# A first stage in two passes of four units, with twelve modulation tiles on TensorE

## The chip, the cores and the metric

The kernel runs on one core of one Trainium2 chip. The metric is the device time of one execution in microseconds. Engines are called TensorE (PE in the profile, PEld for its weight loads), VectorE (DVE), ScalarE (ACT), GpSimd (POOL) and SyncE (SP, whose queue issues the DMAs).

## What is computed

Two residual blocks over 512 tokens of width 2048, the first with two layers and a context of 256 tokens. All of it is fp32. Cut to what the change touches:

```
for l in range(DEPTH):
    sh_l, sc_l, g_l = jnp.split(jax.nn.silu(c) @ w_mod[l] + b_mod[l], 3, axis=-1)
    sh_c, sc_c, g_c = jnp.split(jax.nn.silu(c_ctx) @ w_mod[l] + b_mod[l], 3, axis=-1)
    hl = xl * (1.0 + sc_l[:, None, :]) + sh_l[:, None, :]
    hc = xc * (1.0 + sc_c) + sh_c
    parts_l = jnp.split(hl @ w_in[l], SPLIT_POINTS, axis=-1)
    ...
y_conv = jax.nn.silu(g) * (b_gate * conv3(c_gate * u))
y_pool = jax.nn.silu(g) * (einsum(window_mean(u) - u, pool_w) * pool_scale)
out = jnp.concatenate([y_conv, y_attn, y_pool], axis=-1) @ w_out_l
```

A shift, scale or gate is a vector of 2048 numbers per sequence: a product of silu(c) with a 2048x6144 matrix. The columns of that matrix come in 48 tiles of 128 (0 to 15 shift, 16 to 31 scale, 32 to 47 gate).

## The kernel before

**Matrix products.** Every fp32 operand of a product is split into a high part (a cast to fp32r) and a low part (the rest), and a product is three matmuls: high by high, high by low, low by high. A *unit* is one tile of 128 columns of `w_in`: 16 k-steps, in each three matmuls over the 512 rows of the latent sequence (into `u.lat`) and three over the 256 rows of the context (into `u.cx`). `load_chunk` fetches the weights: DMA to `wraw` on SyncE's queue, cast to `whi` on ScalarE, subtraction to `wlo` on GpSimd. `H[k]` and `Hc[k]` hold the rows in both parts.

**Dots.** A modulation value is a dot of 2048 numbers per partition. In the first stage `gemv` and `dot` make them from a whole tile `wm` (128x2048 fp32, 1 MB): one operation with a running sum on VectorE (L292), or, for the second vector of every odd tile, a product on GpSimd (L288) and a sum on ScalarE (L289). Later stages do them in quarters of 512 in the background (`dots`, `along`: so many steps per finished unit, put late by the scheduler): on GpSimd and ScalarE during attention (L797, L798), on VectorE in the conv and pool branch (L801).

**The first stage** (`pool("start")`, 0 to 325 us) runs three passes over the 16 k-steps. Pass 1, five units (the gates of the four pool tiles and the first conv gate): per k-step two dots for the scale, the rows times (1 + scale) without the shift (L743), split into parts (L713 and L139), then `side_steps` with the matmuls (L240 latent, L241 context). The missing shift is added to those gates later: `pgb` holds the product of the shift with the gate columns. Pass 2, three units (the other conv gates), no new rows; the 32 dots of the shift run beside it. Pass 3 adds the shift to the rows (L761), splits them again, and makes the four units of head 0. The gates go to DRAM (`PGd`) through `pg` (L754, L755).

**Attention of layer 0** (to about 1084 us): 27 units and eight heads; in the background the eight gates' shift products and 16 tiles of layer 0.

**The branch** (to about 1358 us) goes conv 0, pool 0, conv 1, pool 1, conv 2, pool 2, pool 3, conv 3. A conv tile j has units j (copied to `uu`), 8+j (times `uu` into `V`, three taps into `yc`) and 4+j (times `yc`), then its gate from DRAM (`early_gate`, L499), tanh, a last product (L530) and `yc` to DRAM. A pool tile sums windows on GpSimd, makes `dd` (L560, L561), casts to `dh` on ScalarE (L564), makes `dl` on GpSimd, and multiplies by `pool_w` on TensorE into `ps_v`; `yp` (L579) takes that out. `dd` and `yp` share the one buffer of `yc`, `U` that of `V`. PSUM has four `ps_m` buffers, two per unit with context.

The order on each engine is set when the program is built, by a scheduler with priorities; each engine then runs its own queue in order.

## Time and profile before

| what | us |
|---|---|
| median of three runs | 3625.3 (3614.6 to 3630.26) |
| the profiled execution | 3616.4 |
| its span, first to last instruction | 3614.7 |
| TensorE busy | 3270.7 |
| VectorE busy | 2482.0 |
| first stage | 0 to 325.3 |
| branch of layer 0 | 1083.8 to 1358.0 |

Busy times are of one execution. Matmuls are pipelined and their ends are modelled, so the time of a stretch of matmuls is read from the starts of two of them and not from their lengths. A group with "idle before" shows what the engine waited for ahead of these instructions. PEclk is the granted clock of TensorE as a share of 2.4 GHz (its other level is 1.2 GHz).

### The profile page before, as it was taken

The page shows a single profiled execution, that of the slowest core. Times are in us where ns is not written, and L with a number is a line of the kernel's source. Part 1 is how long each engine was busy: PE and PEld are TensorE (multiplying, and loading weights), DVE is VectorE, ACT ScalarE, POOL GpSimd, SP SyncE. Part 2 cuts the span into 40 slices and gives each one's busy share as a digit, 9 for nine tenths or more (in the row PEclk, how much of TensorE's full clock was granted, in tenths as well). Part 3 has the DMA queues.
Part 4 walks back from the last instruction along what each step waited for, and adds up shares of the span by engine and source line. Part 5 has one row for each costly group of instructions (what it writes and reads, how often), then busy time and mean ns, then how long its engine had stood idle before and what let it go on. Part 6 is the DMA issues. An engine that isn't in the chain of part 4 may idle for free.

```text
span 3614.7 us, 47947 instructions
## 1 busy us (share of the span) xinstructions
PE 3270.7 (90%) x16462; PEld 2740.4 (76%) x16462; DVE 2482.0 (69%) x3785; ACT 1545.9 (43%) x3208; POOL 2064.5 (57%) x1452
## 2 busy tenths in 40 slices
PE   5769899989998879889999999999989899999997
PEld 4668788878886767668888888877768787787765
DVE  9994555555547998874466655486477899986676
ACT  4433656666542113233566664322445333245343
POOL 5665677777423443255877773488776544444432
PEclk8889999999999989999999999999999999999998
DMA  7542333333215557664655552487776222223575
GB/s 260 198 174 87 107 108 101 111 107 105 72 65 181 175 162 236 202 212 142 169 148 148 149 149 76 148 302 245 236 225 199 88 87 89 85 82 102 183 223 186
DMA packets 271700, 553.61 MB, mean 153 GB/s; under 512 B 30592, under 2 KB 37600, under 8 KB 263264
## 3 DMA queue, kind: packets, MB, share of 16 engines
q1 hardware_dynamic: 268896, 537.97, 46.3%
q0 software_dynamic: 2560, 12.58, 1.7%
q8 instruction: 129, 2.11, 0.2%
q14 instruction: 115, 0.94, 0.1%
HBM read 508.05 MB, written 29.80 MB: 149 GB/s over the span
## 4 chain that ended last, share of the span: by engine, by line
PE 43%; DVE 27%; DMA 12%; issue 8%; POOL 6%; ACT 5%; SPq 0%; DVEq 0%; POOLq 0%; ACTq 0%
PE ps_m L166 32%; DMA wraw<-in_w_out_dram 5%; DVE acc L980 5%; DVE gpr L801 4%; DVE gjunk L292 2%; POOL gpr L797 2%; DVE wlo L139 2%; PE ps_s L389 2%; POOL wlo L139 2%; PE ps_v L428 2%; DVE h L139 2%; ACT whi L159 2%; DMA gv<-in_cc_dram 1%; DVE wm L292 1%; DVE hf L761 1%
## 5 line engine op out<-in xcount | busy, mean ns | idle before, releaser
L139 POOL TENSOR_TENSOR wlo<-wraw,whi 128x512 fp32r<-128x512 f32 x760 | 1115.6, 1485 | 876.0 <-ACT whi L159 763.3
L166 PE MATMUL ps_m<-h,whi 128*128 128x512 f32 (+1 forms) x4608 | 1569.3, 399 | 36.2 <-ACT vT L355 27.7
L166 PEld LDWEIGHTS ps_m<-h,whi 128*128 128x128 f32 x4608 | 875.4, 192 | 224.3 <-ACT vT L355 30.0
L159 ACT CAST whi<-wraw 128x512 fp32r<-128x512 f32 x1032 | 603.5, 618 | 779.1 <-DMA wraw<-in_w_out_dram 272.8
L166 PE MATMUL ps_m<-h,wlo 128*128 128x512 f32 (+1 forms) x2304 | 916.9, 398 | 0.1
L797 POOL TENSOR_TENSOR gpr<-gw,gv 128x512 f32<-128x512 f32 x320 | 425.3, 1329 | 227.9 <-ACT gpr L798 161.4
L166 PE MATMUL ps_m<-hc,whi 128*128 128x256 f32 x1920 | 518.5, 284 | 0.0
L166 PEld LDWEIGHTS ps_m<-h,wlo 128*128 128x128 f32 x2304 | 442.0, 192 | 93.8 <-POOL wlo L139 0.4
L139 DVE TENSOR_TENSOR wlo<-wraw,whi 128x512 fp32r<-128x512 f32 x272 | 242.5, 905 | 185.2 <-ACT whi L159 184.8
L166 PEld LDWEIGHTS ps_m<-hc,whi 128*128 128x128 f32 x1920 | 359.3, 191 | 3.9
L798 ACT ACTIVATE gpr<-gpr 128x512 f32<-128x512 f32 x320 | 201.9, 631 | 247.3 <-POOL gpr L797 246.6
L166 PE MATMUL ps_m<-hc,wlo 128*128 128x256 f32 x960 | 271.7, 283 | 0.0
L801 DVE SCALAR_TENSOR_TENSOR gpr<-gw,gv 128x512 f32<-128x512 f32 x264 | 255.6, 968 | 11.4 <-DMA gw<-in_w_mod_dram 3.0
L980 DVE SCALAR_TENSOR_TENSOR acc<-gu,pack,acc 128x511 f32<-128x511 f32 (+24 forms) x240 | 232.1, 979 | 5.4
L619 PE MATMUL ps_m<-wlo,y 128*128 128x512 f32 x512 | 206.2, 403 | 21.6 <-POOL wlo L139 12.6
L394 DVE TENSOR_REDUCE mx<-ps_s 128x1 f32<-128x768 f32 (+1 forms) x160 | 134.8, 842 | 114.1 <-PE ps_s L389 112.7
L620 PE MATMUL ps_m<-whi,y 128*128 128x512 f32 x512 | 202.2, 396 | 2.2 <-DVE y L139 1.6
L166 PEld LDWEIGHTS ps_m<-hc,wlo 128*128 128x128 f32 x960 | 183.4, 191 | 0.8
L618 PE MATMUL ps_m<-whi,y 128*128 128x512 f32 x512 | 181.3, 396 | 1.0 <-ACT whi L159 1.0
L423 DVE TENSOR_TENSOR aTl<-ps_t,aTh 128x384 fp32r<-128x384 f32 (+1 forms) x144 | 77.3, 537 | 151.9 <-ACT aTh L422 151.6
L240 PE MATMUL ps_m<-h,whi 128*128 128x512 f32 x320 | 125.4, 439 | 58.9 <-DVE h L139 30.3
L389 PE MATMUL ps_s<-K,Q 128*128 128x384 f32 x576 | 134.2, 348 | 7.9 <-ACT E L403 6.1
(370 smaller groups left out, 5622.0 us busy)
## 6 DMA issues: line engine op xcount, KB each, us to landing
wraw<-in_w_in_dram SPq DMA_DIRECT2D x640, 256.0 KB, 3.0
wraw<-in_w_out_dram SPq DMA_DIRECT2D x384, 256.0 KB, 3.5
wm<-in_w_mod_dram SPq DMA_DIRECT2D x48, 1024.0 KB, 5.8
gw<-in_w_mod_dram SPq DMA_DIRECT2D x192, 256.0 KB, 3.5
gw<-in_w_ada_dram SPq DMA_DIRECT2D x136, 256.0 KB, 3.3
wm<-in_w_ada_dram SPq DMA_DIRECT2D x14, 1024.0 KB, 5.2
K<-K POOLq DMA_DIRECT2D x32, 384.0 KB, 4.1
yraw<-yd SPq DMA_DIRECT2D x40, 256.0 KB, 3.5
```

The lines of the kernel that those rows point to most:

```text
L139: eng.tensor_tensor(lo, src, hi.bitcast(F32), op=ALU.subtract)
L159: nc.scalar.copy(hi[:, sl], raw)
L166: nc.tensor.matmul(ps, w, mv[part], start=(first and p == 0), stop=(last and p == 2))
L389: nc.tensor.matmul(o, Qm[:, q0:q0 + 128], kp[:, c * ncol:(c + 1) * ncol], start=i == 0, stop=i == 1)
L394: nc.vector.reduce_max(mx, sv, axis=AX.XY)
L618: nc.tensor.matmul(ps, yh, hi[:, sl], start=(k == 0), stop=False)
L619: nc.tensor.matmul(ps, yh, lo[:, sl], start=False, stop=False)
L620: nc.tensor.matmul(ps, yl, hi[:, sl], start=False, stop=(k == KT - 1))
L797: nc.gpsimd.tensor_tensor(pr, w, t, op=ALU.mult)
L798: nc.scalar.activation(pr, pr, AF.Copy, scale=scale, accum_out=part[v][:, i:i + 1])
L801: nc.vector.scalar_tensor_tensor(junk, w, scale, t, op0=ALU.mult, op1=ALU.mult, accum_out=part[v][:, i:i + 1])
L980: nc.vector.scalar_tensor_tensor(A[:, s:], U[:, :NL - s], wj(i), A[:, s:], op0=ALU.mult, op1=ALU.add)
```

## The change

The first stage has two passes of four units. Pass 1 makes the four pool gates from the scaled rows, pass 2 the four units of head 0 from shifted rows. The four conv gates become plain units inside `conv_tile`. Twelve of the 32 modulation tiles (0, 4, 8, 12 and the even ones from 16 to 30) are laid out as they stand in `w_mod`, and TensorE makes their 128x2 values for both vectors in 16 fp32 matmuls with two columns each; the other 20 tiles are dots on VectorE for both vectors. In pass 1 the rows are scaled straight into the high part on ScalarE, and the low part is one operation on VectorE (L739 of the new file). In pass 2 the x tiles are loaded a second time, ScalarE scales and shifts them, casts the high part, and the low part goes to VectorE (512 columns) and GpSimd (256). `wm` has four buffers instead of three. Behind it, `pgb` has four gates instead of eight, four tiles of layer 1 move from the branch to attention, and the branch takes 6 background steps per unit instead of 10.

```diff
+PE_TILES = (0, 4, 8, 12) + tuple(range(16, 32, 2))
...
-    GATES = (52, 53, 54, 55, 12, 13, 14, 15)
+    GATES = (52, 53, 54, 55)
...
-        gate = early_gate(xp, 4 + j) if l == 0 else unit(w, 12 + j, H, cx)
+        gate = unit(w, 12 + j, H, cx)
         for o, vo, n in seqs:
             th = xp.tile([128, NL], F32, name="th", tag="th", bufs=2)
-            silu2(th[:, :n], gate[:, o:o + n] if l == 0 else pt(gate, o), th[:, :n])
+            silu2(th[:, :n], pt(gate, o), th[:, :n])
...
-        for p, (g0, n) in enumerate(((0, 5), (5, 3))):
...
-                        dot(sp, wm, (cl, cc_)[i], s1[i], last=i == 1, split=k % 2 == 1)
...
-                    gemv(sp, a["w_mod"][0][k], [(cl, "l0", "b_mod0", k), (cc_, "c0", "b_mod0", k)],
-                         wm_bufs=3, split=k % 2 == 1)
...
+        def columns(m, dst):
+
+            wm = load_gemv(sp, a["w_mod"][0][m], 4)
+            if m in PE_TILES:
+                ps = next(banks)()[:, :2]
+                for q in range(KT):
+                    nc.tensor.matmul(
+                        ps, wm[:, q * 128:(q + 1) * 128], cT[:, 2 * q:2 * q + 2], start=q == 0, stop=q == KT - 1
+                    )
+                return ps
+            if not vecs:
+                vecs.extend(cvecs(sp, 0, 1))
+            for i in range(2):
+                dot(sp, wm, vecs[i], dst[:, i:i + 1], last=i == 1)
+            return dst
...
+        def scaled_rows(k):
+            r = columns(16 + k, s1[:, k])
+            xr = load_x(k)
+            nc.vector.tensor_scalar(s1[:, k], r, P("b_mod0")[:, 16 + k:17 + k], 1.0, op0=ALU.add, op1=ALU.add)
+            for i, (nm, o, n, dst) in enumerate(halves):
+                nc.scalar.activation(dst[k][:, 0], xr[:, o:o + n], AF.Copy, scale=s1[:, k, i:i + 1])
+            for i, (nm, o, n, dst) in enumerate(halves):
                 nc.vector.scalar_tensor_tensor(
+                    dst[k][:, 1], xr[:, o:o + n], s1[:, k, i:i + 1], dst[k][:, 0].bitcast(F32),
+                    op0=ALU.mult, op1=ALU.subtract,
+                )
+
+        def shifted_rows(k):
+            r = columns(k, sh[:, k])
+            xr = load_x(k)
+            hf = sp.tile([128, NT], F32, name="hf0", tag="hf0", bufs=2)
+            nc.vector.tensor_scalar(sh[:, k], r, P("b_mod0")[:, k:k + 1], None, op0=ALU.add)
+            for i, (nm, o, n, dst) in enumerate(halves):
+                nc.scalar.activation(
+                    hf[:, o:o + n], xr[:, o:o + n], AF.Identity, scale=s1[:, k, i:i + 1], bias=sh[:, k, i:i + 1]
+                )
+                nc.scalar.copy(dst[k][:, 0], hf[:, o:o + n])
+                sub_lo(dst[k][:, 1], hf[:, o:o + n], dst[k][:, 0], nc.gpsimd if i else nc.vector)
+
+        def pass_(rows, ns, zero):
+            us, ch = side_units(zero), []
+            rows(0)
+            for k in range(KT):
+                if k < KT - 1:
+                    rows(k + 1)
+                side_steps(w0, ns, us, H, Hc, k, ch, zero)
+            return us
...
+        for g, u in enumerate(pass_(scaled_rows, GATES, zero)):
...
+        us = pass_(shifted_rows, (16, 24, 32, 40), zero)
...
-            dots(ap_, ("sh_l", "sh_c"), 1.0, [a["w_gateT"][g] for g in range(8)], [pgb[:, 0], pgb[:, 1]], 2, 1),
+            dots(ap_, ("sh_l", "sh_c"), 1.0, [a["w_gateT"][g] for g in range(4)], [pgb[:, 0], pgb[:, 1]], 2, 1),
             mod_dots1(ap_, 0, 32, 48, 2, 1),
+            mod_dots1(ap_, 1, 0, 4, 2, 1),
...
-        along(mod_dots1(gp, 1, 0, 20, 4), 10)
+        along(mod_dots1(gp, 1, 4, 20, 4), 6)
...
+    for m in PE_TILES:
+        a["w_mod"][0, m] = v["w_mod"][0][:, m * 128:(m + 1) * 128].reshape(16, 128, 128).transpose(1, 0, 2).reshape(128, 2048)
```

How the order on the engines moves is seen at three places.

VectorE in pass 1, k-steps 1 to 4, before. `gjunk` and `wm` are the outputs of the dots of the two vectors, `h` and `hc` the low parts of latent and context rows, `s` the scale:

```order
L292 SCALAR_TENSOR_TENSOR gjunk,s_389<-wm,ca_171 128x2048
L139 TENSOR_TENSOR hc_1_148<-hf_289,hc_1_148 128x256
L739 TENSOR_SCALAR s_389<-s_389,pk 128x1
L139 TENSOR_TENSOR h_2_133<-hf_339,h_2_133 128x512
L139 TENSOR_TENSOR hc_2_149<-hf_339,hc_2_149 128x256
L292 SCALAR_TENSOR_TENSOR gjunk,s_439<-wm,ca_171 128x2048
L739 TENSOR_SCALAR s_439<-s_439,pk 128x1
L292 SCALAR_TENSOR_TENSOR wm,s_440<-wm,ca_176 128x2048
L292 SCALAR_TENSOR_TENSOR gjunk,s_514<-wm,ca_171 128x2048
L739 TENSOR_SCALAR s_390<-s_390,pk 128x1
L739 TENSOR_SCALAR s_440<-s_440,pk 128x1
L139 TENSOR_TENSOR h_3_134<-hf_388,h_3_134 128x512
```

The same engine and place after; `ps_v` is the column product of a TensorE tile:

```order
L282 SCALAR_TENSOR_TENSOR gjunk,s_174<-wm,ca_216 128x2048
L735 TENSOR_SCALAR s_174<-ps_v,pk 128x2
L282 SCALAR_TENSOR_TENSOR wm,s_174<-wm,ca_219 128x2048
L735 TENSOR_SCALAR s_174<-s_174,pk 128x2
L739 SCALAR_TENSOR_TENSOR h_2_129<-xT,s_174,h_2_129 128x512
L739 SCALAR_TENSOR_TENSOR hc_2_145<-xT,s_174,hc_2_145 128x256
L282 SCALAR_TENSOR_TENSOR gjunk,s_174<-wm,ca_216 128x2048
L739 SCALAR_TENSOR_TENSOR h_3_130<-xT,s_174,h_3_130 128x512
L282 SCALAR_TENSOR_TENSOR wm,s_174<-wm,ca_219 128x2048
L739 SCALAR_TENSOR_TENSOR hc_3_146<-xT,s_174,hc_3_146 128x256
```

Of two k-steps one now has its scale from TensorE, and has no dot on VectorE.

VectorE at the start of the last pass, before. The dots of the shift (`mod`) stand between the shifting of the rows into `hf` and their low parts, and the rows of k-steps 2 and 3 are shifted ahead of a dot:

```order
L139 TENSOR_TENSOR hc_1_148<-hf_1675,hc_1_148 128x256
L300 TENSOR_TENSOR mod_l_163<-mod_l_163,pk 128x1
L761 SCALAR_TENSOR_TENSOR hf_1706<-h_2_133,mod_l_163 128x512
L761 SCALAR_TENSOR_TENSOR hf_1706<-hc_2_149,mod_c_164 128x256
L761 SCALAR_TENSOR_TENSOR hf_1737<-h_3_134,mod_l_163 128x512
L761 SCALAR_TENSOR_TENSOR hf_1737<-hc_3_150,mod_c_164 128x256
L292 SCALAR_TENSOR_TENSOR gjunk,mod_l_163<-wm,ca_171 128x2048
L139 TENSOR_TENSOR h_3_134<-hf_1737,h_3_134 128x512
```

The same after, with the buffers' numbers, from the last two copies of gates (`pg`) to the low part of k-step 1:

```order
L770 COPY pg_1005<-ps_s_180 128x256
L770 COPY pg_1009<-ps_s_180 128x256
L282 SCALAR_TENSOR_TENSOR wm_1438,sh1_175<-wm_1438,ca1_219 128x2048
L748 TENSOR_SCALAR sh1_175<-ps_t_1386,pk_84 128x2
L748 TENSOR_SCALAR sh1_175<-sh1_175,pk_84 128x2
L282 SCALAR_TENSOR_TENSOR gjunk_1500,sh1_175<-wm_1498,ca0_216 128x2048
L282 SCALAR_TENSOR_TENSOR wm_1498,sh1_175<-wm_1498,ca1_219 128x2048
L282 SCALAR_TENSOR_TENSOR gjunk_1540,sh1_175<-wm_1538,ca0_216 128x2048
L748 TENSOR_SCALAR sh1_175<-sh1_175,pk_84 128x2
L140 TENSOR_TENSOR h0_0_127<-hf0_1042,h0_0_127 128x512
L282 SCALAR_TENSOR_TENSOR wm_1538,sh1_175<-wm_1538,ca1_219 128x2048
L140 TENSOR_TENSOR h0_1_128<-hf0_1058,h0_1_128 128x512
```

Four dots stand between the last copy of a gate and the first low part here, and three more between the first copies and these.

TensorE in the branch, around the first product of pool tile 0 (`ps_v<-dh,ph`), before. `ps_m_10254` and `ps_m_10255` are the two halves of conv 1's unit 1, in its k-steps 13 and 14 of 16:

```order
L166 MATMUL ps_m_10254<-h0_13_144,wlo_10315 128x512
L166 MATMUL ps_m_10255<-hc0_13_160,wlo_10315 128x256
L166 MATMUL ps_m_10254<-h0_14_145,whi_10314 128x512
L166 MATMUL ps_v_10240<-dh_10222,ph_10228 128x512
L166 MATMUL ps_m_10255<-hc0_14_161,whi_10314 128x256
```

After. `ps_m_10187` and `ps_m_10188` are conv 1's next unit, 9, in its k-step 2; unit 1 is complete:

```order
L163 MATMUL ps_m_10187<-h0_2_129,whi_10189 128x512
L163 MATMUL ps_m_10188<-hc0_2_145,whi_10189 128x256
L163 MATMUL ps_m_10187<-h0_2_129,whi_10189 128x512
L163 MATMUL ps_v_10005<-dh_9987,ph_9993 128x512
L163 MATMUL ps_m_10188<-hc0_2_145,whi_10189 128x256
```

The product moves from the 14th of 16 steps of one unit to the third step of the next.

## Rows read from the trace of the kernel before

**Rows 1.** The page, engines over the whole span: busy us, share, instructions.

```profile
PE 3270.7 (90%) x16462; PEld 2740.4 (76%) x16462; DVE 2482.0 (69%) x3785; ACT 1545.9 (43%) x3208; POOL 2064.5 (57%) x1452
```

**Rows 2.** Windows of four stretches: length, busy us (instructions), PEclk, DMA, GB/s.

```profile
0.00:325.30 325.30, 235.36 (x1156) 197.50 (x1157) 287.93 (x282) 117.82 (x201) 203.81 (x90) 0.88 0.53 187
325.30:1083.80 758.50, 697.76 (x4073) 615.45 (x4072) 408.74 (x731) 438.97 (x1008) 473.11 (x371) 0.96 0.33 98
1083.80:1358.00 274.20, 221.71 (x1173) 189.77 (x1173) 234.33 (x466) 54.76 (x99) 121.54 (x82) 0.90 0.56 173
1358.00:3614.70 2256.70, 2115.87 (x10066) 1737.64 (x10064) 1550.99 (x2308) 934.30 (x1901) 1266.03 (x910) 0.97 0.52 164
```

**Rows 3.** Windows inside the first stage, columns as before.

```profile
20.00:40.00 20.00, 12.05 (x43) 9.21 (x43) 20.00 (x17) 8.50 (x15) 16.13 (x6) 0.91 0.72 263
...
300.00:320.00 20.00, 20.00 (x116) 17.46 (x115) 1.22 (x12) 2.69 (x6) 5.04 (x4) 1.00 0.31 89
```

**Rows 4.** Groups by line, 0:420 us: busy us, mean ns, idle before.

```profile
L292 DVE SCALAR_TENSOR_TENSOR gjunk<-wm,ca 128x2048 bf16<-128x2048 f32 x32 | 95.1, 2971 | 0.6 <-DMA wm<-in_w_mod_dram 0.6
L288 POOL TENSOR_TENSOR wm<-wm,ca 128x2048 f32<-128x2048 f32 x16 | 82.5, 5157 | 34.2 <-DVE gjunk L292 27.4 <-DVE mod_c L300 6.8
...
L139 DVE TENSOR_TENSOR h<-hf,h 128x512 fp32r<-128x512 f32 x24 | 54.1, 2258 | 1.3 <-ACT h L713 1.2
...
L292 DVE SCALAR_TENSOR_TENSOR wm<-wm,ca 128x2048 f32<-128x2048 f32 x16 | 38.4, 2400 | 0.0
...
L761 DVE SCALAR_TENSOR_TENSOR hf<-hc,mod_c 128x256 f32<-128x256 f32 x16 | 29.6, 1852 | 0.0
...
L418 PE MATMUL ps_t<-ident,E 128*128 128x128 f32 x26 | 4.6, 289 | 0.0
...
L418 PEld LDWEIGHTS ps_t<-ident,E 128*128 128x128 f32 x26 | 3.4, 148 | 0.6
```

**Rows 5.** The same view of DVE alone, 290 to 330 us.

```profile
L761 DVE SCALAR_TENSOR_TENSOR hf<-hc,mod_c 128x256 f32<-128x256 f32 x2 | 2.0, 990 | 0.0
...
L761 DVE SCALAR_TENSOR_TENSOR hf<-h,mod_l 128x512 f32<-128x512 f32 x2 | 1.5, 744 | 0.0
```

**Rows 6.** Chain of waits, 40:60 us: start us, length us.

```profile
40.58 4.84 DVE h L139
...
45.76 2.22 DVE gjunk L292 x2
...
48.01 0.22 DVE s L739
```

**Rows 7.** PE in order of time, end of first stage: start, us.

```profile
323.18 0.40 PE L240 MATMUL ps_m<-h,whi 128*128 128x512 f32 x1
323.42 0.28 PE L241 MATMUL ps_t<-hc,whi 128*128 128x256 f32 x1
...
324.24 0.40 PE L240 MATMUL ps_m<-h,whi 128*128 128x512 f32 x1
```

**Rows 8.** PE in order of time, transposes in head 0: start, us.

```profile
380.11 0.49 PE L418 MATMUL ps_t<-ident,E 128*128 128x128 f32 x3
380.35 0.36 PE L428 MATMUL ps_v<-aTl,Vh 128*128 128x256 f32 x1
```

**Rows 9.** DMA, first 300 us: rate in 40 slices, and total.

```profile
GB/s 261 397 399 306 164 324 158 267 193 260 99 301 232 279 95 265 221 336 63 109 230 263 261 10 341 273 201 39 190 193 0 295 55 231 225 58 66 70 0 151
DMA packets 18766, 59.12 MB, mean 197 GB/s; under 512 B 2206, under 2 KB 4382, under 8 KB 14655
```

**Rows 10.** Groups by line, PE, 1083:1358 us: pool tiles' matmuls.

```profile
L166 PE MATMUL ps_v<-dh,ph 128*128 128x512 f32 x4 | 3.2, 793 | 40.3 <-ACT dh L564 40.3
...
L166 PE MATMUL ps_v<-dh,ph 128*128 128x256 f32 x4 | 1.5, 386 | 9.4 <-DVE yp L579 9.4
```

**Rows 11.** Groups by line, DVE, 1100:1360 us.

```profile
L801 DVE SCALAR_TENSOR_TENSOR gpr<-gw,gv 128x512 f32<-128x512 f32 x160 | 162.3, 1015 | 6.6 <-DMA gw<-in_w_mod_dram 2.9
...
L499 DVE TENSOR_SCALAR pgr<-pgr,pgb 128x256 f32<-128x256 f32 x8 | 7.1, 886 | 0.0
```

More of the change, by code (lines that the diff above doesn't have):

```diff
@@ L133, in mixer_stack_kernel @@
     PUd = {e: dp.tile([128, NT], F32, name=f"pud{e[0]}{e[1]}") for e in EARLY}
-    GATES = (52, 53, 54, 55, 12, 13, 14, 15)
-    PGd = [dp.tile([128, NT], F32, name=f"pgd{g}") for g in range(8)]
+    GATES = (52, 53, 54, 55)
+    PGd = [dp.tile([128, NT], F32, name=f"pgd{g}") for g in range(4)]
     def sub_lo(lo, src, hi, eng):
@@ L207, in unit, with side_units @@
         return u
-    def side_units(n, zero=None):
-        us = [Unit() for _ in range(n)]
+    def side_units(zero=None):
+        us = [Unit() for _ in range(4)]
         cs = ps_s()
@@ L230, in side_steps @@
             c, o = q // 2, (q % 2) * 512
-            ch[:] = [
-                load_chunk(*(w[n, c][:, o:o + 512] for n in ns[p:p + 2]), narrow=xp if len(ns) - p == 1 else None)
-                for p in range(0, len(ns), 2)
-            ]
+            ch[:] = [load_chunk(*(w[n, c][:, o:o + 512] for n in ns[p:p + 2])) for p in (0, 2)]
         for j, u in enumerate(us):
@@ L240, in side_steps @@
                 nc.tensor.matmul(u.lat, wt, H[k][:, part], start=first, stop=last)
-                nc.tensor.matmul(
-                    u.cx, wt, Hc[k][:, part], start=first and not u.shared, stop=last and not u.shared
-                )
-        if k == KT - 1 and us[0].close is not None:
+                nc.tensor.matmul(u.cx, wt, Hc[k][:, part], start=first and not u.bank, stop=last and not u.bank)
+        if k == KT - 1 and us[0].bank is not None:
             for b in range(2):
-                nc.tensor.matmul(us[0].close[:, b], zero[:, :128], zero, start=False, stop=True)
+                nc.tensor.matmul(us[0].bank[:, b], zero[:, :128], zero, start=False, stop=True)
     def silu2(dst, src, tmp):
@@ L700, in mixer_stack_kernel @@
     new_mod("c1")
-    pgb = const.tile([128, 2, 8], F32, name="pgb")
+    pgb = const.tile([128, 2, 4], F32, name="pgb")
     w0 = a["w_in"][0]
@@ L757, in mixer_stack_kernel @@
-        ns, us, ch = (16, 24, 32, 40), side_units(4), []
-        for k in range(KT):
-            hf = sp.tile([128, NT], F32, name="hf0", tag="hf0", bufs=2)
+        vecs, banks = [], itertools.cycle((ps_t, ps_v))
+        def columns(m, dst):
[9 more added lines that the diff above has]
+                vecs.extend(cvecs(sp, 0, 1))
+            for i in range(2):
+                dot(sp, wm, vecs[i], dst[:, i:i + 1], last=i == 1)
+            return dst
@@ new lines, in pass_ @@
+        def pass_(rows, ns, zero):
[7 more added lines that the diff above has]
+        for g, u in enumerate(pass_(scaled_rows, GATES, zero)):
+            pg = sp.tile([128, NT], F32, name="pg", tag="hf0", bufs=2)
+            nc.scalar.copy(pg[:, :NL], u.lat)
+            nc.vector.tensor_copy(pg[:, NL:], u.cx)
+            nc.sync.dma_start(PGd[g], pg)
@@ L767, in mixer_stack_kernel @@
+        us = pass_(shifted_rows, (16, 24, 32, 40), zero)
+        for i, (nm, o, n, dst) in enumerate(halves):
+            nc.vector.tensor_copy(mods[nm][:, :16], sh[:, :, i])
         derive_constants()
```

81 lines of the change are left out of this document (23 added, 58 removed).

## The prediction

> **What bounds the kernel now.** I read the whole-span line of the page, then a table of windows, then the groups and the order of time inside the two stretches that the change touches. TensorE is busy 90% of the span [rows 1], so at first sight little but TensorE counts. The windows correct that: the loss is uneven [rows 2]. In the first stage (0 to 325.3 us) TensorE is busy 235 of 325 us at a granted clock of 0.88, and VectorE 288. In head 0 to 7 and from the first w_out on, TensorE is busy 92 and 94%. In the conv and pool branch (1083.8 to 1358.0) it is busy 222 of 274 us.
>
> How much of 325 us is matmul work? Near the end of the stage the weights change every pair and nothing waits: six matmuls, three of 512 and three of 256 columns, begin within 324.24 - 323.18 = 1.06 us [rows 7], so a pair takes 0.353 us, and a unit (16 k-steps of three pairs) 17.0 us. Twelve early units are 204 us. The other 121 us are waits and half clock. What ends the waits is VectorE: it is busy 20.0 of the 20 us from 20 to 40, while TensorE has 12, and only at 300 to 320 does that turn round [rows 3]. Its load is the dots of the modulation (128x2048 each, 2.4 and 2.97 us on average) and the low halves (2.26 us for 128x512) [rows 4]. Both are stretched: the chain has 2.22 us for a dot with its read and, five microseconds earlier, 4.84 us for a subtraction [rows 6], while GpSimd runs its own 128x2048 products of 5.16 us [rows 4]. At 290 to 330 us, when those are over, a 128x512 operation with three operands takes 0.74 us [rows 5]. So: **first stage, bound by VectorE; its last 30 us by TensorE.**
>
> In the branch, VectorE is busy 234 of 274 us [rows 2], and a table of averages would name it. The groups say otherwise: TensorE waits 40.3 us before the first product of the four pool tiles, for ScalarE's cast of dh, and 9.4 us before the second, for VectorE's yp [rows 10]. That is 49.7 of its 52.5 idle us: a chain of latencies (gate, yc to DRAM, dd on GpSimd, dh on ScalarE), in front of an in-order queue.
>
> **The change, part by part.** The sum is made against the profiled execution, 3616.4 us; the median of the three runs is 3625.3, so 8.9 us are added at the end.
>
> *VectorE in the first stage.* Before, 48 dots lie on it and 16 on GpSimd. After, 20 of 32 tiles have both dots on VectorE: 40, none on GpSimd. One costs between 2.22 us [rows 6] and 2.97 us [rows 4]: 89 to 119. I take 2.6 (104), since GpSimd's long products go but its 128x512 subtractions stay. The first pass has 16 pairs of low halves (512 and 256 columns, scaled and subtracted in one operation): a pair takes 0.74 + 0.99 = 1.73 us [rows 5], at most twice the 1.85 us of the small one among GpSimd's products [rows 4], 28 to 59; I take 35. The second pass leaves VectorE 16 subtractions of 128x512, the narrow ones go to GpSimd: 0.74 [rows 5] to 2.26 us [rows 4], 12 to 36; I take 24. The 32 bias additions of 0.22 us [rows 6], the silu of the two vectors and four copies of gates are about 15. Sum 178 (144 to 229). The first vector has landed some 12 us in, an estimate from the first 397 GB/s slices [rows 9] and 4.6 MB queued ahead. So VectorE would be through at 190 (156 to 241).
>
> *TensorE in the first stage.* Eight units are 136 us. The twelve column tiles are new: 16 fp32 matmuls of two columns each, and the built program holds two weight loads and two matmuls for each, so 32 pairs per tile, 384 in all. The trace has no such matmul. The nearest row is a transpose, whose weights are 128x128 fp32 too: three begin in 0.24 us, 0.080 us each [rows 8]. Unpipelined, one would be 0.289 + 0.148 = 0.437 us [rows 4]. I take 0.080, because the tile is 32 in a row: 2.6 us per tile, 31 us in all (upper bound 168). A cost below that is excluded: the weights must be loaded. With about 20 us ahead of the first real matmul, 20 + 136 + 31 = 187.
>
> The Trainium skill, page "FP8 and Floating Point Precision", section "TensorE Precision Notes", says that true fp32 takes four passes through the array. No row here shows a pass count. If each of the two matmuls were two passes with a load of its own, a tile would be 64 x 0.080 = 5.1 us and the twelve would be 61 instead of 31: that is the third rival.
>
> *The seam.* The second pass rewrites the rows which the first still reads, and ScalarE's queue has the four gate copies ahead of the first shifted row, so nothing of the second pass overlaps the end of the first. Behind the seam VectorE's order has seven dots (18 us at 2.6) between the copies of the gates and the first low half, and seven more up to the low half of k-step 6, where before the last pass had its rows prepared two steps ahead. TensorE can only run the high halves of steps 0 and 1 meanwhile. I put 20 us on it. TensorE: 207; with VectorE's 190 that leaves few gaps, and I take the end of the stage at **210** instead of 325.3: **-115** (156 + seam on the good side is about 185; 241 on the bad, 250 with a tail).
>
> *DMA.* Bytes stay: the x tiles are loaded twice (+6.3 MB), four gate units less (-4.2 MB) with their stores (-1.6). So 59 MB [rows 9] must come in 210 us, 281 GB/s; single slices reach 399 [rows 9]. Taken at nothing, since 59/0.399 is 148 us; what it costs otherwise is in the second rival.
>
> *Conv gates.* Four units of 17.0 us become plain units of the branch: 68 us of TensorE. Against it: 32 of the 160 dots leave VectorE (35 us at 1.015 us and a read each [rows 11]), and half of the 16 bias additions on the stored gates (0.89 us [rows 11]). Both are off the waiting chain: the 40.3 us hang on ScalarE's dh [rows 10], and the order shows that chain after the new gate as it was after the old product, with tanh and one more product in it, and 19 dots ahead of that product in tile 0. The cover in front of the wait grows by about 5 us in two tiles, since the pool product now stands behind a whole unit and more. So I take 10 of the 68 as absorbed: **+58**. Bounds: 19, if all 49.7 us of waiting go under the units; 78, if the dots ahead of the gates push the chain back by 5 us in two tiles.
>
> *Attention of layer 0.* GpSimd's dots stay 96 steps: half of the gates go, four tiles of layer 1 come. A third list means four more loads of a vector pair with tanh. GpSimd is busy 473 of 758 us there and TensorE 698 [rows 2], so I cost it at nothing; without that cover it would be some 20 us. The 2257 us after the branch [rows 2] keep their work.
>
> Sum: 3616.4 - 115 + 58 = 3559; with 8.9 for the median, **3568 us**.
>
> **The rivals.** (1) *The gates vanish in the branch's waits*, the low bound of that term: -115 + 19 gives 3529. For it: 52 us are idle there, and VectorE gets lighter. Against: they are waits of an in-order queue on a chain that the change doesn't shorten. (2) *The stage stays at the price of a crowded VectorE, or the loads don't keep up*: 250 us by the upper bounds, the same as 59 MB at 236 GB/s, near the 263 that a busy stretch shows [rows 3]; -75 + 58 gives 3608. (3) *Each of the two matmuls of a column product runs twice, with its load*: 64 x 0.080 = 5.1 us a tile [rows 8], 30 us more of TensorE, of which some 25 show, since TensorE is the later of the two engines: -90 + 58 gives 3593. Against it: the built program has two. (4) *Slower: the column matmuls don't overlap their weight loads.* At 0.437 us a pair [rows 4] the twelve tiles take 168 us, 137 more than taken: the stage ends at 347, +22 + 58 gives 3705. For it: with two columns there is no streaming to hide a load behind, and half clock doubles all of it. Against: the transposes' 0.080 us [rows 8]. It decides from 0.28 us a pair on: then 75 us are lost, and with them the gain and half a per cent more.
>
> **How the numbers follow.** About 0.5%, 18 us, is what a measurement of this kernel can tell from no change. Forecast 0.57, rival 1 0.15, rival 2 0.17, rival 3 0.06, rival 4 0.05. Faster than 3607: the forecast but for 0.01, all of rival 1, 0.05 of rival 3, and 0.07 of rival 2, whose time lies at the limit: 0.83. Same: 0.12. Slower: rival 4, 0.05. The range, 3520 to 3620, holds the forecast and both neighbours but for about half of rival 1 below, a third of rival 2 above, and rival 4: 0.18 left out.
>
> **What would show it.** Right: the last matmul of the first stage near 210 us and VectorE no longer full throughout it; column matmuls some 80 ns apart; a gap of 15 to 20 us in TensorE between the passes, with dots on VectorE in it; a branch of about 330 us, still with tens of microseconds before the pool tiles' products. Wrong: a branch under 300 (rival 1); a first stage of 250 with VectorE full or loads late (2); pairs of 160 ns a matmul (3) or over 280 (4).

## The result

The changed kernel takes 3580.3 us (median of four runs, 3576.8 to 3585.0) against 3620.0 us before (3614.4 to 3630.3): a ratio of 0.9891, 95% interval 0.9876 to 0.9905. It is faster by 1.1%; the forecast was 3568 us, faster by 1.6%, with a range of 3520 to 3620. The profiled execution took 3577.6 us with a span of 3575.8.

### The profile page after: what moved, and what is told of

The parts are those of the page before. It is cut to its first block, busy times and chain, and to the rows that moved or that the text cites. A ratio compares the mean times of both kernels' runs of the same rounds, so it can differ in the third digit from the quotient of the medians.

```text
span 3575.8 us, 48562 instructions
## 1 busy us (share of the span) xinstructions
PE 3301.2 (92%) x16850; PEld 2791.3 (78%) x16850; DVE 2324.2 (65%) x3649; ACT 1519.0 (42%) x3181; POOL 1958.8 (55%) x1436
## 4 chain that ended last, share of the span: by engine, by line
PE 49%; DVE 18%; DMA 12%; issue 8%; POOL 7%; ACT 6%; SPq 0%; DVEq 0%; POOLq 0%; ACTq 0%
PE ps_m L163 35%; DVE acc L989 5%; DMA wraw<-in_w_out_dram 5%; POOL wlo L140 3%; POOL gpr L805 3%; DVE gpr L809 2%; PE ps_m L232 2%; PE ps_s L379 2%; ACT whi L156 2%; DVE wlo L140 2%; PE ps_v L418 2%; DMA gw<-in_w_ada_dram 1%; PE ps_s L233 1%; PE ps_m L609 1%; DMA gv<-in_cc_dram 1%
## 5 line engine op out<-in xcount | busy, mean ns | idle before, releaser
L163 PE MATMUL ps_m<-h,whi 128*128 128x512 f32 (+1 forms) x4736 | 1611.2, 398 | 47.3 <-ACT vT L345 32.5
L163 PEld LDWEIGHTS ps_m<-h,whi 128*128 128x128 f32 x4736 | 899.9, 192 | 233.7 <-ACT vT L345 34.1
L163 PE MATMUL ps_m<-h,wlo 128*128 128x512 f32 (+1 forms) x2368 | 940.0, 397 | 0.1
L163 PE MATMUL ps_m<-hc,whi 128*128 128x256 f32 x2048 | 554.5, 283 | 0.0
L163 PEld LDWEIGHTS ps_m<-h,wlo 128*128 128x128 f32 x2368 | 455.1, 192 | 93.8 <-POOL wlo L140 0.8
L163 PEld LDWEIGHTS ps_m<-hc,whi 128*128 128x128 f32 x2048 | 381.0, 190 | 3.4
L163 PE MATMUL ps_m<-hc,wlo 128*128 128x256 f32 x1024 | 288.9, 282 | 0.0
L609 PE MATMUL ps_m<-wlo,y 128*128 128x512 f32 x512 | 208.1, 407 | 21.2 <-POOL wlo L140 13.6
L809 DVE SCALAR_TENSOR_TENSOR gpr<-gw,gv 128x512 f32<-128x512 f32 x232 | 220.7, 951 | 8.4 <-DMA gw<-in_w_ada_dram 2.0
L163 PEld LDWEIGHTS ps_m<-hc,wlo 128*128 128x128 f32 x1024 | 194.9, 190 | 1.0
L609 PEld LDWEIGHTS ps_m<-wlo,y 128*128 128x128 f32 x512 | 98.0, 191 | 56.5 <-POOL wlo L140 22.1
```

What stands on the lines that cost most here:

```text
L163: nc.tensor.matmul(ps, w, mv[part], start=(first and p == 0), stop=(last and p == 2))
L609: nc.tensor.matmul(ps, yh, lo[:, sl], start=False, stop=False)
L809: nc.vector.scalar_tensor_tensor(junk, w, scale, t, op0=ALU.mult, op1=ALU.mult, accum_out=part[v][:, i:i + 1])
```

## The profile after

Windows of the changed kernel over the stretches of [rows 2], cut at the last matmul of the first stage, at the first unit of the branch and at the first matmul of w_out (length, busy us of PE, PEld, DVE, ACT and POOL with instructions, PEclk, DMA, GB/s):

```profile
0.00:238.00 238.00, 209.81 (x1159) 186.82 (x1160) 157.09 (x202) 79.45 (x149) 78.27 (x58) 0.86 0.71 256
238.00:1008.30 770.30, 699.71 (x4074) 618.52 (x4074) 416.54 (x747) 442.08 (x1017) 473.16 (x371) 0.95 0.35 100
1008.30:1318.90 310.60, 280.24 (x1543) 242.05 (x1543) 193.97 (x390) 61.40 (x112) 137.50 (x97) 0.94 0.48 148
1318.90:3575.80 2256.90, 2111.42 (x10079) 1743.87 (x10078) 1556.64 (x2311) 936.07 (x1905) 1269.87 (x911) 0.97 0.52 164
```

The branch of before ends by the same mark at 1354.8, so its stretches are 325.3, 758.5, 271.0 and 2259.9 us. The change is -87.3 in the first stage, +11.8 in the attention, +39.6 in the branch, -3.0 in the rest: -38.9. The prediction had -115, 0, +58 and 0, which is -57. **The total came out nearly right because two terms were off in opposite directions**, and a third, taken at nothing, ate 12 us: the stage was taken 28 us too short and the branch 18 too long. That the sum lands within 12 us of the measured time is luck. VectorE is no longer the full engine of the first stage (288 of 325 us before, 157 of 238 now), TensorE is (210 of 238).

Inside the first stage, four windows: start, first pass, seam, second pass.

```profile
20.00:40.00 20.00, 17.36 (x66) 15.52 (x67) 14.69 (x14) 5.01 (x10) 10.24 (x5) 0.69 0.87 336
40.00:136.50 96.50, 95.33 (x570) 85.58 (x569) 73.96 (x87) 23.05 (x43) 21.78 (x15) 0.89 0.78 278
136.50:162.80 26.30, 13.74 (x77) 12.83 (x75) 21.93 (x26) 4.16 (x8) 8.63 (x4) 0.57 0.89 340
162.80:238.00 75.20, 75.20 (x417) 65.48 (x418) 38.78 (x55) 39.73 (x78) 36.92 (x30) 0.94 0.48 156
```

From the first unit matmul (20.2 us) the first pass lasts 116 us; the prediction had 68 + 21 = 89. The seam is 26.6 us instead of 20. The second pass is 74.8 instead of 78. Those three make 30 us, and the prediction had taken 210 for its sum of 207: the stage missed by 28.

**Column products.** TensorE in order of time, around half a tile at half clock and a whole one at full clock (start, length):

```profile
33.44 3.41 PE L716 MATMUL ps_v<-cT,wm 128*128 128x2 f32 x16
36.70 0.77 PE L232 MATMUL ps_m<-h,whi 128*128 128x512 f32 x1
...
64.32 0.28 PE L233 MATMUL ps_s<-hc,wlo 128*128 128x256 f32 x1
64.44 3.63 PE L716 MATMUL ps_t<-cT,wm 128*128 128x2 f32 x32
67.93 0.47 PE L232 MATMUL ps_m<-h,whi 128*128 128x512 f32 x1
```

A tile is 32 matmuls, as the built program said, but it takes 67.93 - 64.44 = 3.49 us, 0.109 us each, not 0.080. At half clock sixteen take 3.26 us, 0.204 each. The 0.080 was a misreading of [rows 8]: there the 0.24 us from the start of three transposes to the start of the next group were divided by three, but that next matmul begins right behind the third transpose. The same stretch of the kernel before, cut off before the third, has

```profile
380.11 0.38 PE L418 MATMUL ps_t<-ident,E 128*128 128x128 f32 x2
```

Two transposes end 0.38 us after the start and three end 0.49 us after it [rows 8], and all three have the same length, so they stand 0.11 us apart. A transpose with 128 columns and a column product with two cost the same at full clock. What they share is a load of 128x128 fp32 weights for each matmul; that this load is what sets the spacing is argued, and no run parts it. The Trainium skill, page "TensorE: Matmul & The Clock Gate", section "LDWEIGHTS (loading the stationary operand)", gives a load as its number of columns over 1.2, in ns: an estimate of 107 for 128 columns. Both full-clock rows agree, and the half-clock row is beyond it.

**The clock.** Windows at the start of the pass, around that tile, and around two short runs of the same matmuls at 125.3 (14) and 127.9 us (12):

```profile
24.00:28.00 4.00, 1.74 (x8) 1.12 (x6) 3.96 (x3) 0.00 (x0) 4.00 (x2) 0.97 0.97 391
28.00:32.00 4.00, 3.85 (x17) 3.75 (x18) 3.21 (x4) 1.12 (x2) 1.34 (x2) 0.50 1.01 364
...
64.00:68.00 4.00, 4.00 (x38) 3.95 (x36) 4.00 (x5) 0.00 (x0) 1.48 (x1) 1.00 1.01 395
68.00:72.00 4.00, 4.00 (x13) 3.20 (x13) 4.00 (x7) 0.00 (x0) 0.00 (x0) 0.59 0.93 358
...
84.00:88.00 4.00, 4.00 (x14) 3.42 (x14) 3.96 (x8) 0.00 (x0) 0.00 (x0) 0.50 0.97 382
...
124.00:128.00 4.00, 4.00 (x30) 3.66 (x28) 2.56 (x5) 0.32 (x1) 0.00 (x0) 1.00 0.94 316
128.00:132.00 4.00, 4.00 (x30) 3.67 (x29) 2.65 (x3) 0.00 (x0) 0.00 (x0) 1.00 1.01 396
```

In the windows from 64 us on TensorE is busy 4.00 of 4.00 us, yet behind 32 column matmuls in a row the granted clock is 0.59 (mostly the 1.2 GHz level), behind 46 in a row (from 77.96 us on) it is 0.50, and behind 14 and 12 it is 1.00. From 20 to 137 us the mean is 0.85: some 17 us lost. Not all of that stands behind column products alone. Some 10 of the 17 us are lost from 28 to 44 us and from 112 to 120, where TensorE had also waited: it was busy 1.74 of 4.00 us from 24 to 28, and 2.83 of 4.00 from 112 to 116. So 116 us are 68 of units, 28 for about eight tiles at 3.49, 17 of half clock and 3 of waits.

**The seam.** What ScalarE and TensorE waited for, 0 to 240 us (us in total, times, longest):

```profile
ACT pg L769 <- DMA pgd<-pg: 15.5, 2, 13.7
...
PE ps_m L232 <- ACT h L753: 7.3, 1, 7.3
ACT hf L750 <- DMA pgd<-pg: 6.6, 1, 6.6
```

The four gate copies use the two buffers of the shifted rows. The third copy waits for the first stores to land, behind 1 MB loads, and the first shifted row waits for the last ones. Of the 13.7 us, some 4 pass before the first store is issued, at 142.0 us, since VectorE copies its part of a gate behind dots. Meanwhile TensorE makes 70 column matmuls of the second pass, at a granted clock of 0.57. The prediction named the queue of copies and the dots, and missed this wait.

**VectorE** (groups by line, 0 to 232 us): the operations were as sized, or cheaper.

```profile
L282 DVE SCALAR_TENSOR_TENSOR wm<-wm,ca 128x2048 f32<-128x2048 f32 x20 | 48.2, 2410 | 0.2
L282 DVE SCALAR_TENSOR_TENSOR gjunk<-wm,ca 128x2048 bf16<-128x2048 f32 x20 | 48.0, 2401 | 10.2 <-DMA wm<-in_w_mod_dram 10.1
L739 DVE SCALAR_TENSOR_TENSOR h<-xT,s,h 128x512 fp32r<-128x512 f32 x16 | 17.0, 1063 | 5.3 <-ACT h L737 5.3
L140 DVE TENSOR_TENSOR h<-hf,h 128x512 fp32r<-128x512 f32 x16 | 15.6, 980 | 14.3 <-ACT h L753 14.2
L739 DVE SCALAR_TENSOR_TENSOR hc<-xT,s,hc 128x256 fp32r<-128x256 f32 x16 | 10.7, 668 | 0.0
```

A dot is 2.40 us instead of the 2.6 assumed, a pair of low halves 1.06 + 0.67 = 1.73 us (27.7 us in all, not 35), a subtraction 0.98 (15.6, not 24).

**The branch**, groups on PE, 1008.3 to 1318.9 us, against [rows 10]:

```profile
L163 PE MATMUL ps_v<-dh,ph 128*128 128x512 f32 x4 | 2.4, 594 | 25.2 <-ACT dh L554 25.2
...
L163 PE MATMUL ps_v<-dh,ph 128*128 128x256 f32 x4 | 1.5, 382 | 2.3 <-DVE yp L569 2.3
```

27.5 us of waits in two tiles, where before it was 49.7 in four; the two late tiles wait no more.

## The experiments

The theory from the profile after: the first pass is short of TensorE, for the price of the column products and the half clock behind them; the seam is the shared buffer; the branch grew by the gates less what waits and lighter dots gave back. The rivals: VectorE paces the first stage whatever TensorE does, and the gates alone cost what the branch grew. Stretches of each run by the same marks (us, from one profiled execution each; attention begins at the last matmul of the stage), with the median of the timed runs (the kernel before, timed beside each group of them, had medians of 3611 to 3620 us):

| kernel | first stage | attention | branch | rest | time |
|---|---|---|---|---|---|
| before | 325.0 | 758.8 | 271.0 | 2259.9 | 3620.0 |
| changed | 237.6 | 770.7 | 310.6 | 2256.9 | 3580.3 |
| b_gates | 323.5 | 761.7 | 319.8 | 2257.8 | 3663.6 |
| a_dots20 | 230.9 | 764.1 | 320.6 | 2256.7 | 3580.2 |
| a_cols1 | 231.8 | 766.9 | 310.8 | 2258.2 | 3564.8 |
| a_cols2 | 299.3 | 778.6 | 307.7 | 2256.0 | 3647.1 |
| a_dve | 243.4 | 782.0 | 310.8 | 2268.1 | 3603.3 |
| a_spread | 227.5 | 768.5 | 312.8 | 2260.4 | 3573.4 |
| a_pgq | 237.4 | 770.8 | 312.3 | 2259.8 | 3586.0 |
| a_spread_pgq | 230.1 | 778.4 | 310.3 | 2263.4 | 3585.1 |
| a_pgw | 238.4 | 759.6 | 311.1 | 2262.4 | 3573.8 |
| a_spread_pgw | 228.0 | 772.1 | 309.7 | 2262.5 | 3575.9 |
| a_s8_pgw | 224.4 | 758.6 | 311.8 | 2263.4 | 3560.6 |
| a_bal | 229.2 | 778.4 | 311.6 | 2266.9 | 3587.2 |

**The gates alone, in the kernel before** (b_gates):

```diff
-        gate = early_gate(xp, 4 + j) if l == 0 else unit(w, 12 + j, H, cx)
+        gate = unit(w, 12 + j, H, cx)
```

> The kernel before with one edit: the conv tiles of layer 0 take their gate from a plain unit of the branch. The first stage still makes and stores the four early conv gates, which nothing reads any more, and all dots stay where they were. So this is the branch's part of the change without its lighter VectorE. Theory A (the prediction's term: 68 us of units less 10 absorbed, so the 39 us that the changed kernel's branch grew are 58 for the gates less some 19 for the dots that went elsewhere): branch 271 to about 329 us, time 3620 to about 3676. Theory B (the gates alone cost what was measured, the waits before the pool products take the rest): branch about 310 us, time about 3659. The waits of TensorE before the four pool products tell the two apart: about 40 to 50 us as before under A, under 30 under B.

The branch is 319.8 us, between the two: the gates cost +48.8. TensorE's waits before the pool products, in this kernel:

```profile
L166 PE MATMUL ps_v<-dh,ph 128*128 128x512 f32 x4 | 2.8, 694 | 33.2 <-ACT dh L564 33.2
...
L166 PE MATMUL ps_v<-dh,ph 128*128 128x256 f32 x4 | 1.3, 334 | 2.9 <-DVE yp L579 2.9
```

They fall from 49.7 to 36.1, so the longer cover takes 13.6 us of four waits; in all 19 of the 68 are absorbed, not 10. Part of the rest is the clock: the granted clock of the branch is 0.95 here and was 0.90, and TensorE's busy time in it grows by 60 us and not by 68. Time 3663.6, ratio to before 1.0143 (1.0125 to 1.0160).

**The four tiles of dots back in the branch** (a_dots20):

```diff
-            mod_dots1(ap_, 1, 0, 4, 2, 1),
-        along(mod_dots1(gp, 1, 4, 20, 4), 6)
+        along(mod_dots1(gp, 1, 0, 20, 4), 10)
```

> The changed kernel with one edit taken back: the first four modulation tiles of layer 1 (16 steps of dots) lie in the branch again, at ten steps a unit as before, and not behind the attention of layer 0. Theory A (those tiles lengthen the attention, which is 770.3 us in the changed kernel and 758.5 before): attention about 758, branch about 325 instead of 310.5, time about 3583. Theory B (the attention's 12 us are not these tiles): attention about 770, branch about 325, time about 3595. Theory C (VectorE's load doesn't set the branch): branch about 310, time at or below 3580.

The branch is 320.6, 10 us longer, as theories A and B had it in direction: the lighter VectorE is worth 10 there, and 48.8 - 10 is the measured 39.6 to within a microsecond. Of the 10 us, 7.1 are a wait before the third pool tile's first product, which the changed kernel doesn't have. The edit changes the number of dots (160 for 128) and their pace (ten steps a unit for six) together, so the run doesn't part these. The attention, 764.1, decides nothing, for the reason at the end of this section.

This run also tells how far one trace of the first stage can be trusted. Its edit lies behind the stage, and in both traces the instructions of the stage stand in the same order on every engine; yet the stage took 230.9 us here and 237.6 in the changed kernel, 5 of the 7 us in the first pass (111 for 116). From 20 to 137 us it has

```profile
20.00:137.00 117.00, 114.17 (x673) 103.52 (x671) 92.69 (x105) 27.97 (x52) 37.51 (x21) 0.88 0.81 300
```

so a granted clock of 0.88, where the changed kernel had 0.85. A difference of 7 us in the stage between two runs is therefore not clear of what one order of instructions shows by itself.

**Column products nearly taken away, and doubled** (a_cols1, a_cols2):

```diff
-                for q in range(KT):
+                for q in range(1):                      a_cols1
+                for q in [*range(KT), *range(KT)]:      a_cols2
```

> The changed kernel with the twelve column products cut to the first of their 16 k-steps; the other 15 of 16 are left out, so the modulation is incomplete; everything else, loads included, is there. Theory A (the column products and the half clock behind them hold up the first pass): 8 tiles x 3.3 us plus up to 17 us of half clock come out of the first pass, the stage ends at 195 to 210 instead of 238, time 3540 to 3550. Theory B (VectorE or the loads pace the pass all the same, the products only fill their gaps): the stage ends at 225 or later, time 3566 or more.

> The changed kernel with each column product run twice into the same bank (the second overwrites the first), so TensorE has 384 more matmuls of two columns in the first stage, 0.109 us each at full clock (32 in 3.49 us in the changed kernel) and 0.204 at half. Theory A (TensorE is one of two nearly equal limits of the first pass, the other is VectorE: with the products almost gone the stage was only 6 us shorter): all twelve tiles show, 12 x 3.5 to 12 x 5 us, stage 280 to 298 instead of 238, time 3620 to 3640. Theory B (VectorE alone paces the first stage, the products lie in TensorE's gaps): stage under 258, time under 3600.

Nearly without them the stage is 6 us shorter than in the changed kernel, which can't be told from nothing (in a_dots20 it was 7 us shorter with all of them); with twice as many it is 62 us longer (time 3647.1, slower than before by 0.8%, interval 0.6 to 1.0). Theory B of the first run holds in the stage (its time, 3564.8, lies 1 us below that theory's bound), and theory A of the second, a little beyond its ranges: a kink. The window from 20 to 137 us, about the first pass, in the changed kernel and in a_cols1:

```profile
20.00:137.00 117.00, 113.19 (x636) 101.56 (x637) 89.15 (x100) 28.56 (x53) 32.52 (x19) 0.85 0.80 289
```

```profile
20.00:137.00 117.00, 83.34 (x386) 68.52 (x384) 108.70 (x121) 24.77 (x45) 43.30 (x18) 0.83 0.92 348
```

TensorE goes from 113 to 83 us, VectorE from 89 to 109 of 117. The whole first pass doesn't get shorter but longer, 121 us for 116; the 6 us come from the seam (21.0) and the second pass (70.7). What TensorE waits for in a_cols1, 18 to 145 us:

```profile
PE ps_m L232 <- DVE h L739: 25.2, 6, 7.4
PE ps_m L232 <- ACT whi L156: 11.3, 1, 11.3
```

By the order built for this run VectorE does dots of the second pass ahead of the low halves of the first, and TensorE waits for these. So with the products nearly gone VectorE, in that order, limits the pass, and taking them away earns nothing that these runs can tell. Whether another order of the same work would be faster stays open. The granted clock is no better without them either: 0.83, with TensorE idle for 34 of the 117 us. Upward, a tile costs 62 / 12 = 5.1 us: 3.5 at full clock, the rest for the most part lost clock (0.78 in the first pass of a_cols2).

**All 32 tiles on VectorE** (a_dve): `PE_TILES = ()`.

> The changed kernel with no tile on TensorE: all 32 modulation tiles of the first stage are dots on VectorE (64 instead of 40). Theory A (24 dots of 2.4 us, 58 us, make VectorE the bound: 157 + 58 us of work and a start at 12 us): the stage ends at 240 to 255 and VectorE is full in it, time 3580 to 3597; so the column products earn little, since TensorE pays 42 us and some half clock for them. Theory B (the products on TensorE carry the gain of the stage): the stage ends at 270 or later, time over 3610. Theory C (the products cost more than they bring): the stage ends before 235, time under 3575.

The stage is 243.4, only 6 us longer than with twelve tiles on TensorE (12 against a_dots20): theory A in the stage. VectorE is full from the first unit matmul on, busy 209 of 218 us:

```profile
25.40:243.40 218.00, 159.59 (x761) 131.33 (x762) 208.97 (x223) 69.16 (x131) 109.04 (x48) 0.89 0.68 239
```

So of the 87 us by which the change shortened the stage, 82 are there without a single tile on TensorE. They come from its other parts, four units fewer in the stage and less work for VectorE and GpSimd in it; no run parts these two, but VectorE's busy time in the stage falls from 288 to 226 us with them. The time, 3603.3, lies between the forecasts of theories A and B: in the profiled executions another 22 us lie in the attention and the rest, where its code is that of the changed kernel.

**Products handed out in fours** (a_spread):

```diff
             for p, (wt, part) in enumerate(((hi, 0), (hi, 1), (lo, 0))):
...
+            if between:
+                between(4)
...
-                if k < KT - 1:
-                    rows(k + 1)
-                side_steps(w0, ns, us, H, Hc, k, ch, zero)
+                r = rows(k + 2) if k < KT - 2 else iter((0,))
+                next(r)
+                side_steps(w0, ns, us, H, Hc, k, ch, zero, some)
+                next(r, None)
```

> The changed kernel with the sixteen k-steps of a column product handed out in fours behind the units of the step before, and rows prepared two steps ahead, so that TensorE has fewer long runs of two-column matmuls. Theory A (runs of 22 and more of them drop the clock: 0.59 in the 4 us behind the run at 64.4, 0.50 in those behind the run at 78.0): the granted clock of 20 to 137 us rises from 0.85 to over 0.92, the first pass takes 100 to 108 us instead of 116, time 3566 to 3574. Theory B (the clock falls from waits, and VectorE's order of dots and low halves sets the pace): clock below 0.88, first pass 112 or more, time 3576 or more.

```profile
20.00:137.00 117.00, 114.78 (x681) 104.44 (x681) 100.44 (x109) 30.01 (x54) 44.41 (x22) 0.90 0.86 312
```

The clock is 0.90 (between the two forecasts), the first pass 103 us instead of 116, the time 3573.4. The four builds with the products in one piece (the changed kernel, a_dots20, a_pgq and a_pgw) have clocks of 0.85 to 0.88 in this window and first passes of 111 to 116 us, so the pass is 8 to 13 us shorter, with 4 us given back at the start, and the rise of the clock is small. The length fits theory A, the clock only in part; and rows were also prepared a step earlier, and this run doesn't part the two.

**The stores of the seam on GpSimd's queue** (a_pgq, and a_spread_pgq with both edits):

```diff
-            nc.sync.dma_start(PGd[g], pg)
+            nc.gpsimd.dma_start(PGd[g], pg)
```

> The changed kernel with the four stores of gates at the seam put on GpSimd's queue instead of SyncE's, where they lay behind loads of 1 MB. Theory A (ScalarE's wait of 13.7 us for the first pair of stores, and of 6.6 us for the second, hold up the first shifted row, as two buffers serve both the gates and the rows): the seam shrinks from 26.6 to 10 to 16 us, time 3564 to 3570. Theory B (VectorE's seven dots between the passes hold it up as well; GpSimd's queue is as slow): seam 22 or more, time 3575 or more.

> Both edits at once: column products handed out in fours two steps ahead, and the gate stores on GpSimd's queue. If both theories A hold and add, the stage ends at 212 to 222 instead of 238 and the time is 3552 to 3562. If VectorE paces both places, the stage ends at 232 or later and the time is 3573 or more.

```profile
ACT pg L769 <- DMA pgd<-pg: 18.4, 2, 16.5
...
POOL pgd L771 <- DVE sh L748: 7.1, 1, 7.1
```

These are waits of a_pgq, 120 to 180 us. Theory A fell: the seam is 33 us. The stores still take their time, 7.3 us in the median from issue to landing (8.6 in the changed kernel), and the issue now waits on GpSimd too. With both edits, a_spread_pgq, the first pass is 103 us as in a_spread and the seam 26.2; the stage, 230.1, lies near the second forecast's bound and the time, 3585.1, inside it. The Trainium skill, page "DMA: Bandwidth & Descriptors", section "Issuing engines are not separate DMA queues", says that DMAs of all engines run on the same 16 engines and that another issuer saves its own issue time only. The trace fits that: the DMA share of 137 to 163 us is 0.89 in the changed kernel and 0.96 in a_pgq, and the longest wait went from 13.7 to 16.5 us.

**Gates copied into the modulation buffers** (a_pgw, and a_spread_pgw with the products in fours):

```diff
-            pg = sp.tile([128, NT], F32, name="pg", tag="hf0", bufs=2)
+            if g % 2 == 0:
+                pair = sp.tile([128, D], F32, name="pg", tag="wm", bufs=4)
+            pg = pair[:, g % 2 * NT:(g % 2 + 1) * NT]
```

> The changed kernel with the gates at the seam copied into two buffers of the modulation tiles (two gates in each) instead of the two buffers of the shifted rows; the stores stay on SyncE's queue, and ScalarE's copies and the first shifted rows no longer wait for a store to land. Those two waits were 13.7 and 6.6 us in the changed kernel; the built program has two dots between the copies and the first low half now, where it had seven. Theory A (the shared buffer is what makes the seam 26.6 us): seam 8 to 16 us, stage 224 to 230 unless the second pass waits for its dots, time 3563 to 3572. Theory B (the seam is VectorE's and the loads' backlog, which only moves into the second pass): seam shorter, second pass 80 us or longer instead of 74.8, stage 234 or later, time 3575 or more.

> The same seam with the column products handed out in fours two steps ahead, which had brought the first pass from 116 to 103 us. If both add: stage 212 to 220, time 3553 to 3563. If VectorE's backlog decides (it is busy 100 of the first pass's last 117 us): stage 225 or later, time 3570 or more.

The seam shrinks from 26.6 to 12.1 us, and the second pass grows from 74.8 to 96.4: the stage ends at 238.4, as before the edit. Windows of a_pgw:

```profile
140.00:160.00 20.00, 18.05 (x91) 15.69 (x92) 17.30 (x19) 7.27 (x15) 5.80 (x4) 0.76 0.97 378
160.00:180.00 20.00, 17.55 (x97) 15.26 (x97) 20.00 (x18) 8.35 (x16) 14.81 (x8) 0.79 0.84 316
180.00:200.00 20.00, 19.39 (x110) 17.09 (x109) 19.97 (x22) 7.88 (x15) 7.71 (x4) 0.83 0.73 263
```

VectorE is full there: dots that it used to do in the first pass and inside the seam (busy 88 and 22 us there in the changed kernel, 65 and 7 here) now stand in the second pass (79 us instead of 39). Their loads come later, since the gates hold two of the four buffers; no run gave the gates buffers of their own. This is theory B, though the time, 3573.8, lies 1 us below its bound. In a_spread_pgw the first pass is 93.8 us (clock 0.93), the seam 10.2, the second pass 98.5: a gain of 22 in the first is given back in the last; the stage, 228.0, and the time, 3575.9, are those forecast for a VectorE that decides.

**Another share of tiles, with both edits** (a_s8_pgw: 4 of TensorE's tiles in each pass; a_bal: 5 and 6):

> As the run with both edits, and only 8 of the 32 modulation tiles on TensorE instead of 12 (4 of the first pass's 16): 8 more dots on VectorE, 20 us, against 4 tiles of 3.5 to 5 us on TensorE. Theory A (VectorE is the tighter of the two limits once the runs are spread): first pass 110 us or longer, time 8 us or more above that run. Theory B (TensorE is): first pass under 100, time below that run.

> As the run with 8 tiles on TensorE, products handed out in fours and gates copied into the modulation buffers, but with 11 tiles on TensorE, five in the first pass and six in the second (there 4 and 4): VectorE, which was busy 20.0 of 20 us from 140 to 180 us of that run's second pass, gives up two of its 12 tiles there, and TensorE takes about 3.5 us for each. Theory A (in the second pass the dots on VectorE are the limit, 93.9 us for 68 us of units): second pass 80 to 90, stage 210 to 218, and the time follows the stage but for the attention, whose length was 774 to 797 us in ten kernels with the same code there: 3546 to 3560 if it is short as in that run, up to 3575 if long. Theory B (TensorE's clock and the loads limit the second pass as well): second pass 92 or longer, stage 224 or later.

a_s8_pgw has the best time of all: 3560.6 us, ratio to before 0.9843 (0.9824 to 0.9863). Its first pass is 100.5 us, between the two forecasts, its stage 224.4. Against the changed kernel 13 us of the gain are the stage; 12 are the attention, which no edit touched, and the branch and the rest gave back 8. Of the stage's 13 us, 7 are no more than the changed kernel and a_dots20 differ by. a_bal's second pass stays at 95.9 and its stage at 229.2 (theory B), with VectorE at 15.4 of 20 us from 180 to 200, where it had 19.9; its attention is long, and so the time is 3587.2. (The 774 to 797 us in its expectation count up to the first copy of `uu`, 15.4 us later than this table.)

**The attention's spread.** Eleven builds (the changed kernel and all runs from it but a_dots20) have the same code there and take 758.6 to 782.0 us, 771 on average. The builds differ in the order of instructions: the scheduler lays the whole program out anew after any edit ahead of it. The 11.8 us by which the changed kernel's attention is longer lie inside that spread. The two builds with the old code have 758.8 and 761.7, so a part may belong to the change; that stays open, the more so as those two have one and the same order of instructions there and count as one sample. That the order makes most of the spread fits the pairs that share one: these two lie 3 us apart, and a_cols2 and a_spread_pgq, whose orders differ there by a dozen instructions, have 778.6 and 778.4.

## Why the prediction was right in sum, and where it was not

- **What bounds the first stage**: right. With VectorE's load cut and four units moved out, the stage fell by 87 us, and TensorE was next, as the step "TensorE 207 against VectorE's 190" had it. What it missed is how little the second limit leaves: nearly without column products (a_cols1) the stage is 6 us shorter, no more than two traces of one order differ, and with all tiles on VectorE (a_dve) only 6 to 12 us longer.
- **Column products at 0.080 us from the transposes [rows 8]**: mis-sized by a misreading. The transposes stand 0.11 us apart, and rightly read they would have given the 3.5 us a tile that was measured, 11 us more for the twelve. The price is 0.109 at full clock and 0.204 at half, so a tile is 3.5 us, not 2.6, and with the clock it takes along 5.1. That last figure is rival 3's, by another way: the trace shows 32 matmuls a tile and no second run of any. Rival 4 decided from 0.28 us a pair on; the dearest pairs, at half clock, took 0.204. The neighbour was well chosen; the step that failed was the division.
- **The clock of the first pass**: left out. The sum took units at 17.0 us from a stretch at full clock [rows 7], though the stage before stood at 0.88 [rows 2]; after, the first pass stands at 0.85, some 17 us. It is the largest of the terms that the stage missed.
- **The seam at 20 us**: right in place, 26.6 in size. The step had the order of VectorE and not the buffer shared with the stores; a_pgw shows that this buffer, exchanged for two of the modulation tiles', earns nothing, since VectorE's backlog comes due later.
- **VectorE's terms**: 178 us forecast, 157 busy to 238 us. Dots, low halves and subtractions were each a little dear.
- **DMA at nothing**: only in part. TensorE waited 9.0 us for modulation tiles, and the stores of the seam were slow behind loads.
- **Conv gates at +58**: mis-sized by 9 for the gates (48.8 in b_gates; 19 absorbed, not 10) and 10 for the dots that left the branch, which the step had called off the waiting chain. They were on it: with the gates alone (b_gates) the last pool tile no longer waits and the third waits 7.6 us, and with the lighter VectorE the third doesn't either. The branch's granted clock, 0.90 before and 0.94 after, was left out here too.
- **Attention at nothing**: 11.8 us, within what two builds of the same code differ.
- **Rivals**: rival 1 came in part, as the waits before the pool products fell from 49.7 to 27.5 us; the others did not. Rival 2's 250 us is the nearest to the stage's 238, but neither of its mechanisms is in the trace: VectorE is not full, and TensorE waited 9 us for loads in all. Of the prediction's signs of being right, the VectorE that is no longer full and the waits before the pool products came; the end of the stage near 210 us (238), column matmuls 80 ns apart (109), a gap of 15 to 20 us (26.6) and a branch of about 330 us (311) did not.

## What to carry over

Price a new instruction from the spacing of neighbours of one kind, and leave out the step to the next kind: three transposes in 0.24 us looked like 0.080 each, and were 0.109. When the engine that is relieved and the one that takes its work are both near their limit, moving work between them earns little: twelve tiles on TensorE are worth 6 to 12 us here. A wait that is removed can come back where the other engine's backlog is due. Where a scheduler lays out the whole program anew, compare stretches, not totals, and look first at how far one stretch differs by itself: here the same code differed by 23 us from build to build, and the same order of instructions by 7 us from trace to trace.
